# Local attention in a two-layer decoder trunk: the probabilities' transposes placed later among the products, the second head's further behind the first's

## The chip, the cores and the metric

The kernel runs as one program on 1 core of a Trainium2 chip. The time is that of the device in microseconds (us). Three runs of the kernel before gave 1879.4, 1879.95 and 1882.35 us, a median of 1879.95 us; a fourth run was taken with the hardware profiler, and all rows quoted here are from that execution.

## The reference

A decoder trunk of two layers over 16 meta tokens and 512 tokens, width 1024, in float32. Each layer is a half-step SwiGLU feed-forward net, a token mixer and another half-step feed-forward net, each between two RMS norms. Layer 0 mixes by gated linear attention, layer 1 by sliding-window attention with one set of keys and values. Only the latter is touched here:

```python
q = (hn @ w_q).reshape(B, L, N_KV_HEADS, GROUP, HEAD_DIM)      # 16 heads of 64
...
s = jnp.einsum('bkgnqd,bknsd->bkgnqs', q_blk, k_band)          # band: 16 meta, 128 previous, 128 own keys
...
p = sink_softmax(s, mask, sink_b[None, :, :, None, None, None])
o_real = jnp.einsum('bkgnqs,bknsd->bkgnqd', p.astype(v.dtype), v_band)
...
return o @ w_out
```

## The kernel before, in words

**Data.** Activations lie transposed (128 channels on the partitions, 528 tokens along the free axis, 8 such tiles for 1024 channels). A product against a weight is made of three float32r products (high and low halves, `mm3s`), weights arrive by DMA in pieces of 128x512 (`raw`), and each piece is split into its halves by ScalarE (L237) and VectorE (L238). PSUM is one pool of 8 tiles of 128x512 (`pp`), so every new product needs a tile whose last reader is done.

**An order written by a planner.** Python generators write the program. `Flow` keeps a clock that only the products advance, by an estimate of each one's time (`mm`, `transpose`); after each group of three products `flow.pump()` runs the generators that are due on that clock, and `yield t` in a generator means "go on when the clock is t further". A number in a `yield` is therefore a place among the products of TensorE, not a time on the chip. The scheduler of the framework then orders each engine's instructions, and may move a few of them past each other. Each engine runs its own list strictly in order.

**Sliding-window attention (`swa`, layer 1).** The 16 heads are 8 pairs, u = 0 to 7; the two heads of a pair are e = 0 and 1. For each pair:

- `x_first` and `x_units` make the queries q; pairs 0 to 3 come together, pairs 4 to 7 one after the other in TensorE tiles `x210` to `x213` (24 products each). VectorE and GpSimd rotate them (`rope`, L1035 to L1038).
- `soft(u)`: for four blocks b of 128 queries the scores of both heads (`sc<u>_<e><b>`, 128x144 for b = 0, else 128x272), moved to SBUF with mask and row minimum by VectorE (L1149), exponentials with row sums on ScalarE (L1156). Then `yield SOFT`, the sinks' part (`es`, L1158, L1159), the reciprocal of the sums (L1161, L1162) and the normalising products: the meta columns of both heads on VectorE (`mt`, L1169), the first head's probabilities on VectorE, the second head's on GpSimd (L1172).
- `core(u)`: `yield NORM`, then for each head eight or seven transposes of 128x128 on TensorE (L177) into two PSUM tiles (`pt<u>_<e>` and `pp<u>_<e>`), copied to SBUF by ScalarE (L1191) and VectorE (L1192), and a `yield` after each head; a last `yield 0.6`; then 22 products with the values into one tile `o<u>`, which is split into halves by ScalarE and VectorE (L398, L399).

A pair's `core` starts when its `soft` is done; `soft(u)` waits for `soft(u - 2)`, and from u = 4 on also for `core(u - 3)`. Between these, TensorE has `x211` to `x213` as other work while pairs 0 to 3 run, and the first half of the output projection (`out_proj(so[:4])`, tiles `y`) as soon as the cores 0 to 3 are done; the second half needs cores 4 to 7.

Of the kernel before, what the change touches and what calls it, by code (L numbers as in the profile page):

```python
# [46 lines left out]
WIN = 2 * P + META  # L47
STAGGER = 5.0
SOFT = 3.0
NORM = 3.0  # L50
GAP = 2.2
LAG = 3
NEG = -1e30
# [74 lines left out]
def trunk_kernel(ctx: ExitStack, tc, a, out):  # L128
# [18 lines left out]
    def ps(name):  # L147
        return pp.tile([P, 512], F32, tag="ps", name=name)

    def pair_tile(name, dt=F32R):  # L150
        return hp.tile([P, 2, TOK], dt, tag="pair", name=name)
# [12 lines left out]
    def mm(o, lhs, rhs, start=True, stop=True, onto=False):  # L164
        inst = pe.matmul(o, lhs, rhs, start=start, stop=stop, skip_group_check=onto)  # L165
        n = 1
        for d in rhs.shape[1:]:
            n *= d
        flow.clock += n / 2400 if rhs.dtype == F32R else max(n / 600, 0.12)
        return inst  # L170
# [5 lines left out]
    def transpose(o, src):  # L176
        pe.transpose(o, src, ident)  # L177
        flow.clock += 0.12
# [217 lines left out]
    def split(dst, src, g):  # L396
        o, n = g
        act.activation(dst[:, 0, o : o + n], src, AF.Copy)  # L398
        dve.tensor_tensor(dst[:, 1, o : o + n], src, dst[:, 0, o : o + n].bitcast(F32), op=ALU.subtract)  # L399
# [695 lines left out]
    def swa(x, kv, finish):  # L1095
        kz, vt, vmz = kv
        set_ahead(10)
        with tc.tile_pool(name="ap", bufs=1) as ap:
# [75 lines left out]
            def core(u):  # L1174
                yield softs[u]
                yield NORM
                j = u // 4
                ss, mt = probs[u]
                pt = [pair_tile(f"pt{u}_{e}", F32) for e in range(2)]
                ptm = pt[0][:, 1, 384:512]  # L1180
                pts = []
                for e in range(2):
                    p, p2 = ps(f"pt{u}_{e}"), ps(f"pp{u}_{e}")
                    for b in range(4):
                        transpose(p[:, b * P : (b + 1) * P], ss[e][0][b][:, -P:])
                    for b in range(3):
                        transpose(p2[:, b * P : (b + 1) * P], ss[e][0][b + 1][:, :P])
                    if e == 0:
                        transpose(p2[:, 384:], mt.rearrange("p c m -> p (c m)"))
                    n = 384 if e else 512  # L1190
                    act.activation(pt[e][:, 0, :512], p, AF.Copy)  # L1191
                    dve.tensor_copy(pt[e][:, 1, :n], p2[:, :n])  # L1192
                    pts.append([pt[e][:, i, :m].rearrange("p (b c) -> p b c", c=P) for i, m in ((0, 512), (1, 384))])
                    yield 0.8
                yield 0.6
                o = ps(f"o{u}")
                kvh = [slice((2 * j + e) * 64, (2 * j + e) * 64 + 64) for e in range(2)]
                for b in range(4):
                    oo = [o[64 * e : 64 * e + 64, b * P : (b + 1) * P] for e in range(2)]
                    for e in range(2):  # L1200
                        mm(oo[e], vt[:, b, kvh[e]], pts[e][0][:, b], True, False)
                    for e in range(2):
                        mm(oo[e], vmz[j][:, 4 * e + b], ptm, False, b == 0)
                    for e in range(2 if b else 0):
                        mm(oo[e], vt[:, b - 1, kvh[e]], pts[e][1][:, b - 1], False, True)
                so[u] = pair_tile(f"so{u}")
                split(so[u], o, (META, SEQ))
# [4 lines left out]
            def attend(u, *after):  # L1212
                softs.append(flow.spawn(soft(u, [*after, *softs[max(u - 2, 0) : max(u - 1, 0)]])))
                cores.append(flow.spawn(core(u)))
# [185 lines left out]
```

## Time and profile before

| | |
|---|---|
| median of three runs | 1879.95 us |
| the profiled execution | 1878.16 us |
| its span on the core | 1876.4 us |
| TensorE busy | 1848.5 us (99%) |
| VectorE busy | 1358.9 us (72%) |
| ScalarE busy | 1002.8 us (53%) |
| GpSimd busy | 324.5 us (17%) |
| scores of the first pair begin | 1388.1 us |
| last products with the values begin | 1485.1 us |

The span is counted from the first to the last instruction; 1.76 us of the profiled execution lie around it. The shares are means over all stages. The change touches the stretch from about 1405 to 1485 us, where pairs 0 to 7 go through softmax and transposes, so that stretch is what has to be read. In rows of the timeline, a float32 product shows as two instructions, so 22 products of `o` are 44 rows, and a pair of score products is "x4".

### The profile page before, as it was taken

The page shows a single profiled execution, that of the slowest core. Times are in us where ns is not written, and L with a number is a line of the kernel's source. Part 1 is how long each engine was busy: PE and PEld are TensorE (multiplying, and loading weights), DVE is VectorE, ACT ScalarE, POOL GpSimd, SP SyncE. Part 2 cuts the span into 40 slices and gives each one's busy share as a digit, 9 for nine tenths or more (in the row PEclk, how much of TensorE's full clock was granted, in tenths as well). Part 3 has the DMA queues.
Part 4 walks back from the last instruction along what each step waited for, and adds up shares of the span by engine and source line. Part 5 has one row for each costly group of instructions (what it writes and reads, how often), then busy time and mean ns, then how long its engine had stood idle before and what let it go on. Part 6 is the DMA issues. An engine that isn't in the chain of part 4 may idle for free.

```text
span 1876.4 us, 36945 instructions
## 1 busy us (share of the span) xinstructions
PE 1848.5 (99%) x14218; PEld 1768.2 (94%) x14218; DVE 1358.9 (72%) x2681; ACT 1002.8 (53%) x2181; POOL 324.5 (17%) x378
## 2 busy tenths in 40 slices
PE   8999999999999999999999999999999999999997
PEld 8999999999999999999999898989976898989897
DVE  7884748776574988484789685858799589848584
ACT  6662636564455666262665563636556566636363
POOL 2101010320001310101033001010353131010102
PEclk9999999999999999999999999999999999999999
DMA  5555566322113255555642356565311215656551
GB/s 194 145 154 141 152 149 160 119 68 79 46 58 112 68 131 157 138 148 148 168 159 57 101 153 157 149 156 165 123 57 46 79 46 132 166 147 160 144 147 45
DMA packets 133104, 231.17 MB, mean 123 GB/s; under 512 B 14912, under 2 KB 27584, under 8 KB 132928
## 3 DMA queue, kind: packets, MB, share of 16 engines
q1 hardware_dynamic: 111904, 190.94, 32.3%
q0 software_dynamic: 20736, 37.76, 12.9%
q8 instruction: 111, 1.82, 0.4%
q14 instruction: 65, 0.53, 0.1%
q10 hardware_dynamic: 288, 0.13, 0.0%
HBM read 226.67 MB, written 2.10 MB: 122 GB/s over the span
## 4 chain that ended last, share of the span: by engine, by line
PE 89%; DVE 7%; ACT 2%; issue 1%; POOL 0%; DMA 0%; DVEq 0%; ACTq 0%; POOLq 0%
PE y L165 30%; PE a L165 21%; PE x L165 18%; PE c L165 10%; PE d L165 5%; PE e L165 1%; PE po L165 1%; DVE w L238 1%; PE o L165 1%; DVE H L457 1%; ACT s L1156 0%; PE ps L165 0%; ACT w L237 0%; DVE s L1149 0%; DVE sh_q L1035 0%
## 5 line engine op out<-in xcount | busy, mean ns | idle before, releaser
L270 POOL DMA_DIRECT2D raw<-in_w_in x144 | 126.0, 939 | 973.4 <-DMA raw<-in_w_in 429.4
L165 PE MATMUL y<-hidl0f,w 128*128 128x256 f32 (+1 forms) x2112 | 260.5, 285 | 0.0
L238 DVE TENSOR_TENSOR w<-raw,w 128x512 fp32r<-128x512 f32 x378 | 244.7, 675 | 20.8 <-ACT w L237 18.0
L165 PEld LDWEIGHTS y<-hidl0f,w 128*128 128x128 f32 x2112 | 258.7, 188 | 0.2
L265 DVE TENSOR_TENSOR w_s<-raw,w_s 128x512 fp32r<-128x512 f32 x288 | 195.2, 689 | 80.7 <-ACT w_s L264 78.5
L165 PE MATMUL y<-hidl1f,w 128*128 128x512 f32 (+1 forms) x1344 | 249.0, 346 | 0.0
L165 PEld LDWEIGHTS y<-hidl1f,w 128*128 128x128 f32 x1344 | 212.3, 188 | 33.2 <-DVE w L238 0.3
L264 ACT ACTIVATE w_s<-raw 128x512 fp32r<-128x512 f32 x288 | 177.6, 625 | 111.1 <-DVE raw L280 70.2
L237 ACT ACTIVATE w<-raw 128x512 fp32r<-128x512 f32 x378 | 207.5, 586 | 33.8 <-PE y L165 28.0
L265 DVE TENSOR_TENSOR w<-raw,w 128x512 fp32r<-128x512 f32 x216 | 145.6, 688 | 35.9 <-ACT w L264 34.1
L165 PE MATMUL x<-x_l0m,w 128*128 128x272 f32 (+1 forms) x1200 | 157.8, 288 | 0.0
L264 ACT ACTIVATE w<-raw 128x512 fp32r<-128x512 f32 x216 | 130.6, 621 | 48.0 <-PE y L165 42.2
L587 DVE TENSOR_TENSOR Y<-y,Y 128x256 f32<-128x256 f32 (+2 forms) x176 | 82.1, 473 | 100.4 <-PE y L165 100.1
L165 PEld LDWEIGHTS x<-x_l0m,w 128*128 128x128 f32 x1200 | 149.3, 188 | 1.2
L165 PE MATMUL a<-zl0f_t,w_s 128*128 128x264 f32 x864 | 117.4, 285 | 0.0
L165 PE MATMUL a<-zl1f_t,w_s 128*128 128x256 f32 x864 | 114.3, 281 | 0.8 <-ACT c L783 0.7
L394 POOL TENSOR_TENSOR acc_post<-acc_post,sq_post 128x256 f32<-128x256 f32 (+1 forms) x78 | 65.9, 844 | 282.6 <-ACT sq_post L393 280.2
L165 PEld LDWEIGHTS a<-zl0f_t,w_s 128*128 128x128 f32 x864 | 110.3, 188 | 0.0
L165 PEld LDWEIGHTS a<-zl1f_t,w_s 128*128 128x128 f32 x864 | 106.9, 188 | 1.9 <-ACT c L783 1.8
L165 PE MATMUL x<-x_l0f,w 128*128 128x256 f32 (+1 forms) x768 | 98.2, 289 | 7.6 <-ACT w L237 5.9
L165 PEld LDWEIGHTS x<-x_l0f,w 128*128 128x128 f32 x768 | 96.1, 191 | 8.6 <-ACT w L237 5.9
L165 PE MATMUL x<-x_l1f,w 128*128 128x256 f32 (+1 forms) x576 | 92.3, 320 | 0.0
(368 smaller groups left out, 3319.0 us busy)
## 6 DMA issues: line engine op xcount, KB each, us to landing
raw<-in_w_in SPq DMA_DIRECT2D x424, 256.0 KB, 3.8
raw<-in_w_in POOLq DMA_DIRECT2D x144, 256.0 KB, 5.2
raw<-in_w_out SPq DMA_DIRECT2D x96, 256.0 KB, 3.5
raw<-in_gla_in SPq DMA_DIRECT2D x50, 256.0 KB, 3.2
raw<-in_w_last SPq DMA_DIRECT2D x48, 256.0 KB, 3.5
raw<-in_w_out SPq DMA_DIRECT2D x64, 128.0 KB, 3.0
raw<-in_gla_out SPq DMA_DIRECT2D x16, 256.0 KB, 2.8
raw<-in_w_q SPq DMA_DIRECT2D x16, 256.0 KB, 4.2
```

What stands on the lines that cost most here:

```text
L165: inst = pe.matmul(o, lhs, rhs, start=start, stop=stop, skip_group_check=onto)
L237: act.activation(w[:, 0, :m], raw[:, :m], AF.Copy)
L238: hold(dve.tensor_tensor(w[:, 1, :m], raw[:, :m], w[:, 0, :m].bitcast(F32), op=ALU.subtract))
L264: act.activation(w[:, 0, :512], src, AF.Copy)
L265: dve.tensor_tensor(w[:, 1, :512], src, w[:, 0, :512].bitcast(F32), op=ALU.subtract)
L270: pool.dma_start(dst, src, accum_op=ALU.add)
L394: pool.tensor_tensor(sums[0][:, :n], sums[0][:, :n], t[:, :n], op=ALU.add)
L457: dve.tensor_tensor(h, t, h, op=ALU.add)
L587: dve.tensor_tensor(y, p[:, :n], y, op=ALU.add)
```

## The change

Two numbers of the planner change.

```diff
-NORM = 3.0
+NORM = 4.0
...
                     pts.append([pt[e][:, i, :m].rearrange("p (b c) -> p b c", c=P) for i, m in ((0, 512), (1, 384))])
-                    yield 0.8
+                    yield 0.7 if e else 2.0
                 yield 0.6
```

The first transposes of a pair are placed 1.0 us of planned products later, the second head's 2.0 instead of 0.8 behind the first's, and the products with the values 1.3 instead of 1.4 behind those: 2.1 us of planned products later in all. No instruction is added or removed.

On TensorE, pair 0, before: right behind the last product of the query tile x212 come its first head's transposes.

```order
L165 MATMUL x212_0_17271<-x_l1m_7_16760,w211_1_17268 128x512 x3
L177 MATMUL pt0_0_17372<-ident_73,Y_71 128x128 x4
L177 MATMUL pp0_0_17373<-ident_73,Y_71 128x128 x3
L177 MATMUL pp0_0_17373<-ident_73,mt0_17203 128x128
L165 MATMUL sc2_02_17386<-kz0_12392,q2_17069 128x272
L165 MATMUL sc2_12_17388<-kz0_12392,q2_17069 128x272
L177 MATMUL pt0_1_17405<-ident_73,Y_71 128x128 x4
L177 MATMUL pp0_1_17406<-ident_73,Y_71 128x128 x3
L165 MATMUL sc3_00_17422<-kz0_12392,q2_17069 128x144
```

The same place in the changed kernel, from the same product on:

```order
L165 MATMUL x212_0_17271<-x_l1m_7_16760,w211_1_17268 128x512 x3
L165 MATMUL x213_0_17380<-x_l1m_0_16596,w212_0_17216 128x512 x3
L165 MATMUL sc2_02_17386<-kz0_12392,q2_17069 128x272
L165 MATMUL sc2_12_17388<-kz0_12392,q2_17069 128x272
L177 MATMUL pt0_0_17394<-ident_73,Y_71 128x128 x4
L177 MATMUL pp0_0_17395<-ident_73,Y_71 128x128 x3
L177 MATMUL pp0_0_17395<-ident_73,mt0_17203 128x128
L165 MATMUL sc2_03_17421<-kz0_12392,q2_17069 128x272
L165 MATMUL sc2_13_17423<-kz0_12392,q2_17069 128x272
L165 MATMUL sc3_00_17433<-kz0_12392,q2_17069 128x144
L165 MATMUL sc3_10_17435<-kz0_12392,q2_17069 128x144
L165 MATMUL x213_0_17380<-x_l1m_1_16620,w212_0_17216 128x512 x3
```

Products of x213 and a pair of scores now stand ahead of the first head's transposes, and two pairs of scores and three products of x213 between the two heads'. Since x213 begins here, it is used up earlier. On TensorE before, the transposes of pair 2 stand among products of x213:

```order
L177 MATMUL pp2_0_17575<-ident_73,mt2_17336 128x128
L165 MATMUL x213_0_17538<-x_l1m_2_16640,w212_0_17216 128x512
L177 MATMUL pt2_1_17592<-ident_73,s2_1_17332 128x128 x4
L177 MATMUL pp2_1_17593<-ident_73,s2_1_17332 128x128 x3
L165 MATMUL x213_0_17538<-x_l1m_3_16665,w212_0_17216 128x512 x3
L165 MATMUL x213_0_17538<-x_l1m_4_16690,w212_1_17307 128x512 x3
L165 MATMUL x213_0_17538<-x_l1m_5_16710,w212_1_17307 128x512 x3
```

In the changed kernel they stand among scores of pair 4, and pair 3's first transposes follow ahead of o2:

```order
L177 MATMUL pp2_0_17602<-ident_73,mt2_17336 128x128
L165 MATMUL sc4_00_17638<-kz1_12393,q4_17167 128x144
L165 MATMUL sc4_10_17640<-kz1_12393,q4_17167 128x144
L165 MATMUL sc4_01_17646<-kz1_12393,q4_17167 128x272
L165 MATMUL sc4_11_17648<-kz1_12393,q4_17167 128x272
L177 MATMUL pt2_1_17652<-ident_73,s2_1_17332 128x128 x4
L177 MATMUL pp2_1_17653<-ident_73,s2_1_17332 128x128 x3
L165 MATMUL sc4_02_17665<-kz1_12393,q4_17167 128x272
L165 MATMUL sc4_12_17667<-kz1_12393,q4_17167 128x272
L177 MATMUL pt3_0_17673<-ident_73,s3_0_17427 128x128 x4
L177 MATMUL pp3_0_17674<-ident_73,s3_0_17427 128x128 x3
```

From the end of o1 to the end of o3 TensorE has no product of x213 any more, only scores, transposes and o2, o3; and three pairs of scores (pair 4, blocks 2 and 3, and pair 5, block 1) now stand ahead of the end of o3. The list of VectorE moves with it. Between the normalising of pair 3 (`s3_0`, `mt3`) and the first scores of pair 4 it now reads:

```order
L1172 TENSOR_TENSOR s3_0_17427<-s3_0_17427,den3_17430 128x816
L1169 TENSOR_TENSOR mt3_17432<-s3_1_17428,den3_17430 128x16
L1169 TENSOR_TENSOR mt3_17432<-s3_1_17428,den3_17430 128x48
L1035 STREAM_SHUFFLE sh_q7_16_17627<-x213_0_17380 128x512
L399 TENSOR_TENSOR so1_17596<-o1_17573,so1_17596 128x512
L1192 COPY pt2_0_17599<-pp2_0_17602 128x512
L1036 TENSOR_TENSOR q6_17374<-x213_0_17380,csq_16792 128x512
L1149 ISA s4_0_17632,nm4_17634<-sc4_00_17638,away_16788,nsink_16790 128x144
```

Before, both copies of pair 2 and the split of o1 stood ahead of that normalising, and the splits of two weight pieces (w216) behind it; now it is the other way round. GpSimd's and the DMA queue's lists keep their work: the rotation of pair 6 comes one pair of normalising products earlier on GpSimd, and the loads of weights keep their sequence.

## The prediction

> **What bounds the kernel now.** I began with the page's first part, engine by engine, and went from there to the stretch that the change touches.
>
> ```profile
> PE 1848.5 (99%) x14218; PEld 1768.2 (94%) x14218; DVE 1358.9 (72%) x2681; ACT 1002.8 (53%) x2181; POOL 324.5 (17%) x378
> ```
>
> TensorE (PE) is busy for 99% of the span, so a change of order that adds no instruction can only win or lose TensorE's idle time. The table by stretches (width, then busy time of PE, of its weight loads, of VectorE = DVE, ScalarE = ACT and GpSimd = POOL, then the granted clock) cuts where the program cuts: from the first transposes of pair 0 to the end of o3, from there to the end of o7, and the rest of the output projection.
>
> ```profile
> 1405.40:1438.60 33.20, 29.50 (x298) 22.91 (x296) 30.28 (x93) 18.50 (x59) 14.71 (x12) 1.00 0.16 49
> 1438.60:1485.30 46.70, 45.94 (x371) 35.04 (x370) 31.95 (x106) 27.20 (x83) 7.73 (x8) 1.00 0.11 35
> 1485.30:1512.00 26.70, 26.70 (x212) 25.97 (x211) 17.64 (x38) 16.37 (x35) 9.27 (x12) 1.00 0.32 100
> ```
>
> TensorE is idle for 33.20 - 29.50 = 3.70 us in the first stretch, 0.76 us in the second and not at all in the third: 4.46 us in all, 0.24% of the span. The view of waits says for what:
>
> ```profile
> PE pt L177 <- DVE s L1172: 1.7, 3, 0.9
> PE pt L177 <- POOL s L1172: 0.8, 1, 0.8
> PE pt L177 <- POOL Y L1172: 0.7, 1, 0.7
> PE pp L177 <- ACT pt L1191: 0.5, 1, 0.5
> PE o L165 <- DVE pt L1192: 0.5, 1, 0.5
> PE pt L177 <- DVE nm L1149: 0.2, 1, 0.2
> ```
>
> Nearly all is transposes that wait for normalised probabilities, which later transposes could avoid. But the first stretch has a second reading. DVE is busy for 30.28 us of 33.20 there, and its rows (start, length, operation, idle time ahead) show that it never rests until pair 3 is normalised:
>
> ```profile
> 1410.04 0.68 DVE L238 TENSOR_TENSOR w<-raw,w 128x512 fp32r<-128x512 f32 x1
> 1410.64 0.19 DVE L1162 RECIPROCAL den<-den 128x8 f32<-128x8 f32 x1
> ...
> 1416.68 0.68 DVE L1192 COPY pt<-pp 128x512 f32<-128x512 f32 x1
> ...
> 1418.12 0.55 DVE L1192 COPY pt<-pp 128x384 f32<-128x384 f32 x1
> ...
> 1424.19 0.68 DVE L399 TENSOR_TENSOR so<-o,so 128x512 fp32r<-128x512 f32 x1
> ...
> 1428.29 1.00 DVE L1172 TENSOR_TENSOR s<-s,den 128x816 f32<-128x816 f32 x1
> ...
> 1432.52 0.69 DVE L399 TENSOR_TENSOR so<-o,so 128x512 fp32r<-128x512 f32 x1 [2.40 <-ACT so L398]
> ```
>
> The first idle time is the 2.40 us ahead of 1432.52. So **VectorE sets the pace from 1405 to about 1430 us**, and TensorE's waits there are its queue seen from the other side. Two rows next to each other run into one another by 0.08 us (0.68 from 1410.04, the next at 1410.64), so I count a row's length less 0.08 as its cost.
>
> **The change, part by part.** No instruction comes or goes, and the loads keep their sequence; the cost is waits alone. I follow the changed lists in three steps, against the profiled execution.
>
> *Step 1: when VectorE has normalised pair 3.* Before, at 1428.29 + 1.00 = 1429.29. Ahead of that point the changed list holds two splits of weights more (0.60 each, row 1410.04), and does without pair 2's two copies (0.60 and 0.47, rows 1416.68 and 1418.12) and one split of o1 (0.60, row 1424.19): +1.20 - 1.67 = -0.47. VectorE would be there at 1428.8 if it stays as busy as it was.
>
> *Step 2: when TensorE reaches pair 3's transposes.* Its rows give the price of each piece:
>
> ```profile
> 1405.42 0.63 PE L177 MATMUL pt<-ident,Y 128*128 128x128 f32 x4
> ...
> 1426.91 2.32 PE L165 MATMUL x<-x_l1m,w 128*128 128x512 f32 x9
> 1429.16 0.44 PE L165 MATMUL o<-pt,vt 128*64 128x128 f32 x4
> ...
> 1459.21 0.52 PE L165 MATMUL sc<-kz,q 64*128 64x144 f32 x4
> 1459.66 0.97 PE L165 MATMUL y<-so,w 128*128 128x512 f32 x3
> 1460.56 0.44 PE L165 MATMUL o<-pt,vt 128*64 128x128 f32 x4
> ...
> 1463.11 0.73 PE L165 MATMUL sc<-kz,q 64*128 64x272 f32 x4
> 1463.77 0.66 PE L177 MATMUL pt<-ident,s 128*128 128x128 f32 x4
> ...
> 1464.79 0.73 PE L165 MATMUL sc<-kz,q 64*128 64x272 f32 x4
> 1465.45 0.66 PE L177 MATMUL pt<-ident,s 128*128 128x128 f32 x4
> ...
> 1466.37 0.73 PE L165 MATMUL sc<-kz,q 64*128 64x272 f32 x4
> ```
>
> From start to next start: a query product 0.25 us (nine from 1426.91 to 1429.16), a pair of scores 0.66 (1463.11 to 1463.77) or 0.45 for block 0, transposes of a first head 1.02, of a second 0.92, the 22 products of an o 2.55 (1460.56 to 1463.11). Before, from 1405.42 to the end of o3, these give 24 x 0.25 + 6 x 0.66 + 3 x 0.45 + 4 x 1.94 + 4 x 2.55 = 29.3 us, against 29.50 in the table: the prices hold. In the changed list, between the same start and pair 3's first transposes, stand all 24 products of x213 (6.0), seven pairs of scores and two of block 0 (5.5), the transposes of pairs 0, 1 and 2 (5.8), o0 and o1 (5.1): 22.4 us, so without a wait TensorE would come there at 1427.8. The probabilities are there at 1428.8, and the PSUM tile that these transposes get is one from which VectorE must first have moved pair 4's block 0. The rows for what VectorE does in between:
>
> ```profile
> 1405.37 0.28 DVE L1169 TENSOR_TENSOR mt<-Y,den 128x16 f32<-128x16 f32 x2
> ...
> 1434.34 0.73 DVE L1035 STREAM_SHUFFLE sh_q<-x 128x512 f32<-128x512 f32 x1
> ...
> 1435.48 0.68 DVE L1036 TENSOR_TENSOR q<-x,csq 128x512 f32<-128x512 f32 x1
> 1436.07 0.36 DVE L1149 CUSTOM_DVE_ANT_0 s<-sc,away,nsink 128x144 f32<-128x144 f32 x1
> ...
> 1437.22 0.50 DVE L1149 CUSTOM_DVE_ANT_0 s<-sc,away,nsink 128x272 f32<-128x272 f32 x1
> ```
>
> That is mt 0.20, shuffle 0.65, split of o1 0.60, copy 0.60, rotation 0.60 and two scores 0.57: 3.2 us, to 1432.0. TensorE thus idles for 1432.0 - 1427.8 = **4.2 us instead of 3.70** by then, however the waits are spread: +0.5. Bounds: if the tile comes free elsewhere, 1428.8 decides, 1.0 us of idle, or -2.7; if VectorE itself is held up, later by as much. I take the tile, since the list names that order.
>
> *Step 3: after that.* Behind them stand 1.0 + 2.55 (o2) + 0.66 + 0.92 + 0.45 + 0.66, and o3. VectorE's next copies fit: pair 2's second copy is due at 1432.0 + 0.84 (two scores at 0.42) + 0.47 = 1433.3, o2 starts at 1433.0 and reads it after nine of its 22 products (1.0 us); pair 3's last copy comes about as o3 starts. I count nothing. Past o3, products of the output projection stand among the scores and transposes, and VectorE has 31.95 us of work in 46.70. The 0.76 us of the second stretch (transposes of pairs 4 and 5 next to each other) should go, as pairs 4 and 5 now stand apart: **-0.7**, at worst 0. Behind o7 stand 12 products of the first half of the projection instead of 15: 12 x 0.25 = 3.0 us, and nine small ones, still more than the 1.2 us that the split of o7 takes (0.60 on VectorE by the row of 1424.19, and I take as much for ScalarE): nothing, and 1.2 us if that cover were gone.
>
> The sum is +0.5 - 0.7 = -0.2 us on the profiled execution's 1878.16. That execution is 1.8 us under the median of the runs, so against the median: 1879.95 - 0.2, **about 1879.7 us**. No change that can be measured.
>
> **The rivals.** All turn on VectorE, whose cost is not fixed:
>
> ```profile
> 1411.37 1.22 DVE L1172 TENSOR_TENSOR Y<-Y,den 128x144 f32<-128x144 f32 x2
> ...
> 1416.61 0.15 DVE L1158 TENSOR_TENSOR es<-nm,vec 128x8 f32<-128x8 f32 x1
> ...
> 1420.81 1.02 DVE L1169 TENSOR_TENSOR mt<-s,den 128x16 f32<-128x16 f32 x2
> 1421.75 2.31 DVE L1172 TENSOR_TENSOR s<-s,den 128x144 f32<-128x144 f32 x2
> ...
> 1424.79 1.45 DVE L1158 TENSOR_TENSOR es<-nm,vec 128x8 f32<-128x8 f32 x1
> ```
>
> ```profile
> 1424.29 1.94 POOL L1172 TENSOR_TENSOR s<-s,den 128x144 f32<-128x144 f32 x2 [1.09 <-DVE mt L1169]
> ```
>
> The same tiny es took 0.15 and 1.45 us; the long one ended at 1426.24, when GpSimd's pair of products ended (1424.29 + 1.94 = 1426.23). The normalising pair took 1.22 and 2.31, mt 0.28 and 1.02, each time beside GpSimd. The excess of these three is 1.30 + 1.09 + 0.74 = 3.1 us.
>
> *Faster.* If the new order puts GpSimd's products beside VectorE's copies and scores out of PSUM, that excess goes, VectorE is 3.1 us earlier, the tile decides at 1428.9, and 1.1 us of idle are left: 3.70 - 1.1 = 2.6, with 0.76 behind it 3.4 us, 1876.5; at most all 4.46 us, 1875.5. For it: every wait of the list above is one that a later transpose avoids. Against it: GpSimd has five pairs of products in this stretch either way, and x213's products, that covered pair 2's waits, are spent earlier.
>
> *Slower.* The same holding-up hits VectorE more often. From o1 to o3 TensorE now has no query product, so each us that VectorE is late there is a us on o3. Four more waits like es's at 1424.79 cost 4 x 1.30 = 5.2 us: 1884.9. It decides from three on (3.9 us). For it: rotation and normalising of GpSimd now follow closer on each other. Against it: one row in the old stretch is that bad.
>
> The Trainium skill, "SBUF — State Buffer", section "Who interferes with whom", says that a VectorE instruction with two SBUF inputs is blocked for a whole GpSimd instruction that reads SBUF, while one with at most one SBUF input is not. The rows agree for es; the rule adds that copies out of PSUM are safe, by which the faster rival would be possible, with the same 1876.5.
>
> Against the change speaks "TensorE: Matmul & The Clock Gate" of the Trainium skill, section "What's actually happening": after an idle window of about 3.4 us the clock falls to half. If the 4.2 us of idle came in one piece, an estimate from that page is 1.7 us more, 1881.4. The longest wait in the view above is 0.9 us, with a granted clock of 1.00, and no row shows such a fall.
>
> *That the change does not do what it says* is out: the lists show the moves.
>
> **How the numbers follow.** What a measurement of this kernel can tell from no change is about 0.2%, 3.8 us. My forecast has 0.70, the faster rival 0.18, the slower one 0.12. The faster rival's 1876.5 lies just within 0.2%, its far end at 1875.5 beyond: I give it 0.10 beyond and 0.08 within. So faster by more has 0.10, slower by more 0.12, and within 0.2% 0.78. The range reaches from all idle time gone, 1879.95 - 4.46 = 1875.5, up to three more waits on VectorE, 1879.7 + 3.9 = 1883.6; runs of the kernel before spread by 3 us, so that a part of either rival lies outside.
>
> **What would show it.** Right: in the new profile TensorE is idle for 4 to 5 us from x212's end to o3's, mostly ahead of o0, and of pair 3's transposes, released by DVE's pt (L1192) or nm (L1149) instead of s (L1172); o3 ends near 1440.7; TensorE never waits behind it. Wrong: VectorE with idle time ahead of pair 3's normalising (step 1), normalising long before 1428 or behind 1430 (the rivals), or waits behind o3 (step 3).

## The result, and the profile after

| | before | after |
|---|---|---|
| median of 22 runs each | 1879.05 us (1877.36 to 1882.35) | 1875.9 us (1875.54 to 1877.89) |
| ratio | | 0.9984, 95% interval 0.9979 to 0.999 |
| the profiled execution | 1878.16 us | 1875.54 us |
| the stage (first score product to first product of the next net, `x_l1f`) | 123.88 us | 121.76 us |
| ahead of the stage, unchanged code | 1388.10 us | 1387.50 us |

The change wins 3.1 us between the medians, 0.16%: within 0.2% by the medians, though the interval reaches 0.21%, and not zero. Between the two profiled executions it is 2.62 us, of which 2.12 are in the stage and 0.6 ahead of it, where the code is the same (about 0.1 goes the other way behind it); in all profiles below the stage starts at 1387.4 to 1388.5 whatever the kernel, so I compare stages. For the rest of the 3.1 the clock is the likely cause; the section on the prediction says how far that is shown.

The page's first part after:

```profile
PE 1849.6 (99%) x14218; PEld 1768.5 (94%) x14218; DVE 1354.6 (72%) x2681; ACT 1003.5 (54%) x2181; POOL 323.2 (17%) x378
```

TensorE is busy for 1.1 us more and VectorE for 4.3 us less, with the same instructions. The table by stretches, cut at the same points of the program as in the prediction (the end of `x212`, the end of o3, the end of o7):

```profile
1404.80:1439.32 34.52, 33.62 (x310) 24.67 (x308) 32.20 (x107) 22.57 (x70) 13.37 (x12) 1.00 0.18 55
1439.32:1483.35 44.03, 44.03 (x363) 34.39 (x361) 27.57 (x93) 24.39 (x72) 7.73 (x8) 1.00 0.11 31
1483.35:1509.30 25.95, 25.95 (x209) 25.36 (x208) 17.36 (x38) 15.73 (x34) 9.22 (x12) 1.00 0.31 103
```

TensorE's idle time is 34.52 - 33.62 = 0.90 us, and then none; before it was 3.70 and 0.76. What it waits for in this part:

```profile
PE sc L165 <- DVE q L1036: 0.7, 1, 0.7
PE pt L177 <- DVE pt L1192: 0.2, 1, 0.2
```

No wait for a normalised probability (DVE s, POOL s, POOL Y) is left. The first stretch is now the longer one because work moved into it: 12 pairs of scores stand in it instead of nine. Over the whole stage (width, then TensorE busy), before and after:

```profile
1388.10:1511.98 123.88, 117.94 (x951) 93.68 (x950) 96.98 (x294) 73.85 (x216) 42.22 (x42) 1.00 0.20 63
```

```profile
1387.50:1509.26 121.76, 119.36 (x951) 94.20 (x951) 94.25 (x294) 74.44 (x216) 40.79 (x42) 1.00 0.21 64
```

TensorE's idle time fell from 5.94 to 2.40, by 3.54 us, while its busy time rose by 1.42: together the 2.12. So not all of the idle time that went was won. VectorE did the same 294 rows in 2.73 us less. Cut at the end of o3, with the three pairs of scores that moved counted at 0.66 us each (1.98 us), the part of the stage ahead of it became 0.65 us shorter and the part behind it 1.46: two thirds of the gain lie where pairs 4 to 7 are worked on.

### The profile page after: what moved, and what is told of

It reads as the page before. It is cut to its first block, busy times and chain, and to the rows that moved or that the text cites. A ratio compares the mean times of both kernels' runs of the same rounds, so it can differ in the third digit from the quotient of the medians.

```text
span 1873.7 us, 36947 instructions
## 1 busy us (share of the span) xinstructions
PE 1849.6 (99%) x14218; PEld 1768.5 (94%) x14218; DVE 1354.6 (72%) x2681; ACT 1003.5 (54%) x2181; POOL 323.2 (17%) x378
## 4 chain that ended last, share of the span: by engine, by line
PE 91%; DVE 6%; ACT 2%; issue 1%; DMA 0%; POOL 0%; SPq 0%; DVEq 0%; ACTq 0%; POOLq 0%
PE y L165 30%; PE a L165 22%; PE x L165 18%; PE c L165 10%; PE d L165 5%; PE o L165 1%; PE e L165 1%; PE po L165 1%; DVE w L238 1%; PE sc L165 1%; DVE H L457 1%; PE ps L165 0%; PE pt L177 0%; ACT w L237 0%; DVE Y L587 0%
```

## The experiments

Two theories. **L (hold-up):** VectorE sets the pace of the stage, part of its time is holding still while GpSimd works, and the new order wins by putting GpSimd's products beside other rows. **P (place):** later transposes simply wait less; GpSimd has nothing to do with it. If GpSimd's products are taken out, L says the order wins next to nothing any more, P that it wins the same. Stages are from one profile of each. The kernels were timed in four groups, each on a chip of its own, with the kernel before beside them at 1878.32 (norm_only, gap_only, before_act, after_act), 1878.5 (before_nopool, after_nopool, after_pair, gap_pair), 1877.83 (gap_act, norm_act, after_again) and 1878.77 us (before_again).

| kernel | median us | ratio to before, interval | stage us |
|---|---|---|---|
| norm_only | 1876.8 | 0.999 (0.9982 to 0.9999) | 122.22 |
| gap_only | 1875.33 | 0.9987 (0.9978 to 0.9996) | 121.04 |
| before_act | 1874.99 | 0.9982 (0.9973 to 0.9991) | 121.31 |
| after_act | 1878.05 | 0.9999 (0.999 to 1.0008) | 123.98 |
| before_nopool | 1874.26 | 0.9978 (0.9969 to 0.9986) | 120.31 |
| after_nopool | 1874.03 | 0.9974 (0.9964 to 0.9984) | 122.19 |
| after_pair | 1877.16 | 0.9994 (0.9985 to 1.0003) | 122.54 |
| gap_pair | 1878.88 | 0.9999 (0.999 to 1.0008) | 124.57 |
| gap_act | 1874.49 | 0.9978 (0.9969 to 0.9988) | 120.34 |
| norm_act | 1876.02 | 0.999 (0.9981 to 0.9998) | 122.54 |
| after_again | 1875.84 | 0.9985 (0.9976 to 0.9994) | 121.77 |
| before_again | 1878.15 | 0.9998 (0.9989 to 1.0007) | 127.36 |

### The two halves of the change alone

norm_only has the pair's later start, gap_only the second head's later place:

```diff
-NORM = 3.0
+NORM = 4.0
```

```diff
-                    yield 0.8
+                    yield 0.7 if e else 2.0
```

> Only NORM = 4.0; the gap between a pair's two heads stays at 0.8. Theory P (place: a transpose that stands later waits less, whatever GpSimd does): each of the two edits brings its share of planned time, 1.0 of 2.1 us, so about -1.5 us of the change's -3.1 us in the medians, and the idle time of TensorE from the first transposes to the end of o7 falls from 4.46 us to about 2.5. Theory L (lock: the time is won where GpSimd's products no longer stand beside VectorE's operations on SBUF): no share is due; the time follows the excess of VectorE's rows (es over 0.15, normalising pair over 1.22, mt over 0.28 us), and may be nothing or the whole.

> Only the second head's transposes further behind the first's (2.0 and 0.7 instead of 0.8 and 0.8); NORM stays at 3.0. Theory P: the share of the other 1.1 of 2.1 us, about -1.6 us, TensorE idle about 2.5 us. Theory L: as the excess of VectorE's rows beside GpSimd goes, nothing or the whole; the two parts need not add up to the change.

Measured: the second head's place alone wins 3.0 us (stage -2.84), the pair's later start alone 1.5 us (stage -1.66), both together 3.1 (stage -2.12). Theory P's figure came for the later start (-1.5) and not for the other (-1.6 expected). The halves do not add up: they cure the same loss, and `NORM` on top of the other costs 0.7 us of stage. The second head's place is the part that wins more. It does not do so by less hold-up in total: VectorE is busy for 94.96 us of norm_only's stage and 95.00 of gap_only's, and the stages differ by 1.18 us. Which row is held, and whether TensorE waits behind it, matters too.

### The second head normalised on ScalarE instead of GpSimd

In both kernels, the second head's product of each block with its reciprocal becomes an activation with a scale (four for a pair):

```diff
-                        (pool if e else dve).tensor_tensor(tt, tt, dv.to_broadcast([P, n, w]), op=ALU.mult)
+                        if e == 0:
+                            dve.tensor_tensor(tt, tt, dv.to_broadcast([P, n, w]), op=ALU.mult)
+                        for c in range(b, b + n if e else b):
+                            act.activation(ss[e][0][c], ss[e][0][c], AF.Identity, scale=den[:, e, c : c + 1])
```

> The kernel before, with the second head's probabilities normalised on ScalarE (four activations per pair) instead of GpSimd: GpSimd has only the two rotations left in the stretch. Theory L: VectorE's excess beside GpSimd (1.30 + 1.09 + 0.74 us in three rows) is gone and the kernel gains 2 to 3 us on the kernel before. Theory P: the transposes still stand too early and wait for VectorE; within 1 us of the kernel before, or slower by ScalarE's additional 15 us of work in a stretch of 80.

> The changed kernel with the same move to ScalarE. Theory L: without the lock the change has nothing left to win: within 0.7 us of the run with the order of before and the same move. Theory P: the change is worth its 2 us here as well: 1.5 us or more faster than that run.

before_act wins 2.57 us of stage with the planner's places of before, more than the change does, and 3.3 us in the medians; L had said 2 to 3. after_act is a miss for it: 3 us slower than before_act, no faster than the kernel before. Its waits say part of why:

```profile
PE o L165 <- ACT pt L1194: 1.0, 1, 1.0
PE sc L165 <- ACT pt L1194: 0.5, 1, 0.5
PE sc L165 <- DVE q L1036: 0.3, 1, 0.3
```

TensorE now waits for ScalarE's copies of transposes (`pt`), which stand in ScalarE's list behind the second heads' activations. ScalarE is busy for 85.70 us of this stage instead of 74.44. The waits are not the whole of it: against before_act's stage TensorE's idle time is up by only 0.65 us, its busy time by 2.02, and after_act's timeline shows pairs of scores split between the two heads, each of which costs more (see step 2 below). So the test was not clean: it took one load away and put another in the way. And with the move to ScalarE the scheduler ordered some products of x213 and of o, and some transposes, differently, in before_act as in after_act. Two things followed, leaving the products out without a substitute, and trying each half with ScalarE.

### The second head's products left out

These two kernels leave out the normalising of the second head (the same edit without the activations), so that neither GpSimd nor ScalarE does it. In the stage, TensorE and VectorE run the same sequence of operations as in the kernel before and in the changed kernel.

```diff
-                        (pool if e else dve).tensor_tensor(tt, tt, dv.to_broadcast([P, n, w]), op=ALU.mult)
+                        if e == 0:
+                            dve.tensor_tensor(tt, tt, dv.to_broadcast([P, n, w]), op=ALU.mult)
```

> The kernel before, with the second head's normalising products on GpSimd left out (they are on no other engine either; the second head's probabilities stay unnormalised). Neither GpSimd's lock nor ScalarE's additional work is there. Theory L (the change wins because VectorE is held up 2 to 3 us less beside GpSimd): 2 to 3 us less than the kernel before, as with the move to ScalarE. Theory W (the waits of the transposes for data are what the change removes): the two first-head waits (1.7 us) remain, so at most 1.5 us less than before, from the second heads' 1.5 us.

> The changed kernel with the same products left out. Theory L: within 0.7 us of the order of before with the same omission, or slower than it by what the change costs on TensorE (one pair of scores split by a product of x213, 0.65 us). Theory W: 1.5 to 2 us faster than that run.

The stages (width, TensorE busy, weight loads, VectorE busy) of before_nopool, and then after_nopool:

```profile
1387.40:1507.71 120.31, 116.96 (x950) 93.76 (x950) 91.99 (x294) 73.56 (x216) 25.07 (x26) 1.00 0.21 65
```

```profile
1387.50:1509.69 122.19, 120.28 (x951) 95.02 (x950) 91.55 (x294) 74.28 (x216) 24.74 (x26) 0.99 0.21 64
```

The medians differ by 0.23 us, 1874.26 and 1874.03: without GpSimd's products the order wins nothing that shows. (The longer stage of after_nopool holds a fall of the granted clock, which its 0.99 tells and the last section shows; from the query products at 1389.95 to the twelve score products behind them it is 5.12 us, and 3.59 in the changed kernel. That costs 1.5 us, and 122.19 - 1.5 = 120.7 stands against 120.31.) Theory P is refuted as it was put: the change does not win the same without GpSimd's products. Leaving them out of the order of before wins 4.2 us in the medians and 3.57 of stage, more than L's 2 to 3 and far more than the 1.5 that theory W allowed; in the changed order it shortens the stage by about 1.1 (121.76 to 120.7). The same rows measure the hold-up. VectorE's 294 rows take 96.98 us before and 91.99 without the products, so it was held for 4.99 us; after the change 94.25 - 91.55 = 2.70 are left. The order took away 2.3 us of hold-up, and the stage became 2.12 us shorter; that the two are so alike is not shown to be more than chance, as norm_only and gap_only tell.

One rival these runs do not part from the hold-up. Ahead of o3 the second heads' transposes waited for GpSimd's results themselves (0.7 and 0.8 us in the view of waits before), and leaving the products out takes that wait away as well. How much of the gain ahead of o3 is this direct wait stays open; behind o3 no transpose waits for GpSimd, and step 3 below shows the hold-up there.

### Keeping a pair's score products together

Rows of the new order show some score products of one head alone. Theory S: that split costs time, and ordering the next product behind the pair's second score would win it back. The edit, in after_pair on the changed kernel and in gap_pair on gap_only, is an ordering between two instructions, in `mm` and in `soft`:

```diff
+    scored = [None]
...
+        if scored[0] is not None:
+            after(scored[0], inst)
+            scored[0] = None
...
-                        mm(pst[e][:, :n], qq[rows, META + b * P : META + (b + 1) * P], keys[rows, k0 : k0 + n])
+                        last = mm(pst[e][:, :n], qq[rows, META + b * P : META + (b + 1) * P], keys[rows, k0 : k0 + n])
+                    scored[0] = last
```

> The changed kernel, with the next product ordered behind a pair's second score product, so that the scheduler cannot put a product of x213 between the scores of the two heads (sc3_01 and sc3_11). Theory S (a lone head's score product takes as long as both heads' together, 0.65 us, so a split pair costs 0.65): 0.6 us less than the changed kernel. Rival: the second head's product waits for its PSUM tile just as long, and the time is the same within 0.3 us.

> Only the gap between the heads (NORM = 3.0, 2.0 and 0.7), with the same ordering. Theory S: 0.6 us less than gap_only, about 1874.7 us, the fastest so far. Rival: the same as gap_only within 0.3 us.

S does not hold as a gain: after_pair's stage is 0.78 us longer than the changed kernel's, and its median 1.3 us above that of the changed kernel, which was timed in another group. TensorE's busy time in the stage falls by 0.5 us (119.36 to 118.84), and waits take more than that:

```profile
PE sc L167 <- DVE q L1041: 0.7, 1, 0.7
PE pt L182 <- DVE pt L1198: 0.7, 1, 0.7
PE sc L167 <- DVE nm L1155: 0.4, 1, 0.4
PE o L167 <- DVE nm L1155: 0.4, 1, 0.4
```

By these waits, the split was the scheduler filling a wait for VectorE with something. gap_pair is 3.5 us slower than gap_only, and in its profile nearly all of that is the clock; the last section shows it.

### The halves with ScalarE, and the changed kernel again

gap_act is before_act with the second head's place, norm_act is before_act with `NORM` 4.0 (edits as above), and after_again is the changed kernel, timed beside them.

> The kernel before, with the later place of the second head's transposes (0.7 and 2.0 in place of 0.8) and with the second head normalised on ScalarE instead of GpSimd; NORM stays at 3.0. Theory L (what the change wins is VectorE's hold-up beside GpSimd's products): with those products gone the place wins nothing more, so within 0.7 us of before_act's 1875.0, first score to next net's first product near 121.3 us. Rival Q (with ScalarE as the loaded engine a later place of the second head leaves its transposes and copies behind ScalarE's next activations): 1.5 to 3 us slower than before_act, 1876.5 to 1878, with TensorE waiting for ACT pt and DVE q. Rival P (the place by itself wins): 1 us or more below 1875.0.

> The kernel before, with NORM 4.0 alone and with the second head normalised on ScalarE instead of GpSimd. Theory L: within 0.7 us of before_act's 1875.0. Rival Q, if it is the pair's later start and not the second head's place that loads ScalarE badly: 1.5 us or more slower, 1876.5 to 1878. If gap_act is slow and this is not, the slowness of after_act lies in the second head's place; if neither is, in the two together.

> The changed kernel itself once more, beside the two others, so that all are compared on one chip: 1875.9 us, 3 us below the kernel before. Its profile is a second one of the same code: by theory L the stage from the first score to the next net's first product takes 121.8 us again, within 0.3, unless the granted clock falls behind one of its waits.

gap_act's median is 0.5 us below before_act's, within L's 0.7; but before_act was timed in another group, whose kernel before was 0.5 us slower too, so that against the kernel before the two win the same 3.3 us. Its stage is 0.97 us shorter. norm_act is 1.0 us slower than before_act (stage +1.23), between L's 0.7 and the 1.5 of rival Q, and waits 0.9 us for ScalarE's `pt` ahead of an o, as after_act does. So Q's wait is there with the pair's later start, not with the second head's place, and both halves together are worse (stage +2.67) than their sum. With GpSimd's products the second head's place wins 2.84 us of stage, with ScalarE in their stead 0.97: about two thirds of its gain hang on GpSimd's products, through the hold-up or the direct wait, and the rest is place or the scheduler's different order. after_again repeats the stage to 0.01 us.

**gap_act has the shortest stage of all versions that compute everything; its median is 1.35 us below that of the changed kernel beside it.** Its stage:

```profile
1388.00:1508.34 120.34, 118.69 (x951) 94.11 (x951) 92.12 (x294) 84.87 (x248) 24.91 (x26) 1.00 0.21 65
```

TensorE is idle there for 120.34 - 118.69 = 1.65 us, 1.5 of it in one wait that ends at 1390.5, where the change does not reach.

### The kernel before, profiled again

> The kernel before itself, for a second profile. Its 22 times so far fall into two parts, 1877.4 to 1878.4 and 1878.8 to 1882.4, while the changed kernel's lie nearly all in 1875.4 to 1876.4. Theory H (the granted clock falls to half for one or two stretches of 3.4 us behind the worst waits of the stage, in some executions of it): a profile whose time is over 1879 shows a clock of about 0.5 somewhere in 1386 to 1435 us and a stage as much longer, and one under 1878.5 shows 1.00 throughout and a stage of 123.9 us. Rival (the spread comes from elsewhere, from the loads): a profile over 1879 with a clock of 1.00 in the stage, longer in the lead ahead of it. Theory L says nothing on this; it takes the stage's 2.1 us between the two profiles at 1.00 as what the order wins, and the rest of the 3.1 us between medians as H's.

The profile fell on an execution of 1881.12 us. The table by 5 us (the granted clock is the number ahead of the last two) shows theory H right:

```profile
1385.00:1390.00 5.00, 3.57 (x18) 2.37 (x16) 5.00 (x17) 0.00 (x0) 4.04 (x6) 1.00 0.00 0
1390.00:1395.00 5.00, 4.93 (x13) 3.25 (x13) 3.77 (x11) 2.06 (x8) 4.84 (x5) 0.66 0.56 154
...
1425.00:1430.00 5.00, 3.67 (x18) 3.14 (x19) 4.44 (x12) 1.93 (x4) 1.93 (x2) 0.77 0.00 0
1430.00:1435.00 5.00, 5.00 (x55) 4.09 (x54) 2.08 (x6) 0.12 (x1) 3.20 (x2) 0.89 0.18 56
```

Twice the clock falls behind a stretch with idle time. Its rows at the two places:

```profile
1390.07 3.68 PE L165 MATMUL x<-x_l1m,w 128*128 128x512 f32 x8 [1.50 <-DVE w L238]
...
1427.65 0.90 PE L177 MATMUL pt<-ident,s 128*128 128x128 f32 x3 [0.83 <-POOL s L1172]
1428.35 0.85 PE L177 MATMUL pp<-ident,s 128*128 128x128 f32 x3
1428.85 3.37 PE L165 MATMUL x<-x_l1m,w 128*128 128x512 f32 x9
```

The nine products of 1428.85 took 2.32 in the first profile (the row of 1426.91 in the prediction), the eight of 1390.07 took 2.13 there. From 1390.07 to the twelve score products that follow it is 5.16 us instead of 3.60, and from 1427.65 to the next products with the values 4.50 instead of 2.88: each fall costs 1.6 us, together 3.2 of the 3.48 by which this stage is longer than the first profile's.

## Why the prediction was right where it was, and wrong where it was not

The forecast was 1879.7 us, -0.2 against the median shown then; the change gives -3.1. "Within 0.2%" and the range hold, the likeliest case does not. That "within 0.2%" holds is no merit of the sum, which had the change at nothing: a gain of 3.1 us also lies within 3.8. It is nearly the faster rival's 1876.5 that came.

**What bounds the kernel: right.** VectorE sets the pace up to pair 3's normalising: with TensorE's list as it was, leaving GpSimd's products out shortens VectorE's busy time by 4.99 us and the stage by 3.57 (before_nopool). It is not the only thing that moves the time: gap_act's stage is 0.97 us shorter than before_act's, with VectorE busy as long (92.12 and 92.15 us).

**Step 1 failed**, at the words "if it stays as busy as it was". Pair 3 was to be normalised at 1428.8. To set the changed profile on the clock of the one before I add 0.62 us (the end of `x212`, 1405.42 against 1404.80). VectorE's rows after that show what I had left as it was:

```profile
1410.57 0.80 DVE L1161 TENSOR_TENSOR den<-den,es 128x8 f32<-128x8 f32 x1
...
1414.92 1.00 DVE L1158 TENSOR_TENSOR es<-nm,vec 128x8 f32<-128x8 f32 x1
...
1424.52 0.59 DVE L1158 TENSOR_TENSOR es<-nm,vec 128x8 f32<-128x8 f32 x1
1425.44 0.17 DVE L1161 TENSOR_TENSOR den<-den,es 128x8 f32<-128x8 f32 x1 [0.34 <-ACT es L1159]
...
1426.09 1.23 DVE L1172 TENSOR_TENSOR s<-s,den 128x144 f32<-128x144 f32 x2
```

Pair 3's products end at 1427.3, or 1427.9 on the clock of before: 0.9 us earlier. The normalising pair takes 1.23 and not 2.31, and `mt` never 1.02. Other rows are held instead, shorter: `den` 0.80 against 0.17, es 1.00 and 0.59 against 0.15. Each of the three ends with a GpSimd row:

```profile
1410.06 1.29 POOL L1038 TENSOR_TENSOR q<-q,sh_q 128x512 f32<-128x512 f32 x1
1413.97 1.93 POOL L1172 TENSOR_TENSOR Y<-Y,den 128x144 f32<-128x144 f32 x2 [2.63 <-DVE mt L1169]
1423.00 2.08 POOL L1172 TENSOR_TENSOR s<-s,den 128x144 f32<-128x144 f32 x2 [7.10 <-DVE mt L1169]
```

1410.06 + 1.29 = 1411.35 and 1410.57 + 0.80 = 1411.37; 1415.90 and 1415.92; 1425.08 and 1425.11. In the whole stage the groups shift in the same way, first before, then after (busy time, mean ns of one):

```profile
L238 DVE TENSOR_TENSOR w<-raw,w 128x512 fp32r<-128x512 f32 x29 | 23.7, 832 | 0.7 <-ACT w L237 0.7
...
L1169 DVE TENSOR_TENSOR mt<-s,den 128x16 f32<-128x16 f32 x12 | 4.1, 344 | 0.1
...
L1161 DVE TENSOR_TENSOR den<-den,es 128x8 f32<-128x8 f32 x8 | 1.2, 162 | 1.7 <-ACT es L1159 1.7
```

```profile
L238 DVE TENSOR_TENSOR w<-raw,w 128x512 fp32r<-128x512 f32 x29 | 21.8, 772 | 0.5 <-ACT w L237 0.5
...
L1161 DVE TENSOR_TENSOR den<-den,es 128x8 f32<-128x8 f32 x8 | 3.1, 392 | 1.5 <-ACT es L1159 1.4
...
L1169 DVE TENSOR_TENSOR mt<-s,den 128x16 f32<-128x16 f32 x12 | 2.1, 172 | 0.2
```

The splits of weights take 1.9 us less and `mt` 2.0 less, `den` 1.9 more. The rule that I weighed from the Trainium skill ("SBUF — State Buffer", "Who interferes with whom") thus holds in every row looked at. The faster rival, which had 0.18, named this mechanism, and nearly its idle time ahead of o3 (1.1 us left, measured 0.90). That its 1876.5 lies so near the result is partly luck: ahead of o3 most of the idle time that went came back as busy time, so that 0.65 us were won there instead of its 2.6; behind o3 1.46 were won instead of its 0.76; and about 1.0 of the 3.1 us between the medians lies outside the stage's 2.12. I argued against it that GpSimd has five pairs of products in this stretch either way. It has four (and two rotations), and the argument is beside the point, since what counts is which VectorE row falls beside them.

**Step 2: the kind of wait was named rightly, the places and the size were not.** TensorE does wait behind VectorE's list, but ahead of a score of pair 3 (0.69 us) and of pair 1's transposes (0.18), not ahead of o0 or of pair 3's transposes, and shortly. TensorE's rows after:

```profile
1407.30 1.27 PE L165 MATMUL sc<-kz,q 64*128 64x272 f32 x6
1409.26 0.51 PE L165 MATMUL sc<-kz,q 64*128 64x144 f32 x2 [0.69 <-DVE q L1036]
...
1411.36 0.72 PE L165 MATMUL sc<-kz,q 64*128 64x272 f32 x2
...
1412.51 0.72 PE L165 MATMUL sc<-kz,q 64*128 64x272 f32 x2
...
1429.51 1.21 PE L165 MATMUL sc<-kz,q 64*128 64x272 f32 x4
1430.65 0.66 PE L177 MATMUL pt<-ident,s 128*128 128x128 f32 x4
```

Pair 3's transposes begin at 1430.65, 1431.27 on the clock of before, instead of 1432.0; o3 ends at 1439.32, or 1439.9, instead of 1440.7. Of the 4.2 us of idle that I had by then only 0.90 show, and yet the end of o3 came only 0.8 us earlier than forecast, since TensorE's rows became longer: products of one head alone (x2) take 0.72, as long as both heads' together (x4, 0.73), so a pair whose heads are split costs about 0.65 more, and in the row of 1429.51 (1.21 where a pair costs 0.73) the second head starts only at 1430.00. TensorE is busy for 33.62 us in this part; the 29.50 of before and three more pairs of scores at 0.66 would be 31.48. My prices had no term for these 2.1 us, and after_pair shows that they can't simply be had back.

**Step 3: right that the wait goes, half the size, and another cause.** Nothing waits behind o3, as I said. From o3's end to the end of the stage it took 73.38 us before, and 69.94 after. Three pairs of scores less at 0.66 are 1.98 of the difference; 1.46 are the gain, against the 0.7 that I took. The 0.76 was read from the view of waits, and the rows of the transposes of pairs 4 and 5 before show what that view leaves out:

```profile
1451.14 0.33 PE L177 MATMUL pt<-ident,s 128*128 128x128 f32 x1
1451.66 0.55 PE L177 MATMUL pt<-ident,s 128*128 128x128 f32 x3 [0.19 <-DVE s L1172]
...
1453.92 0.55 PE L177 MATMUL pp<-ident,s 128*128 128x128 f32 x3 [0.49 <-ACT pt L1191]
1454.39 0.73 PE L165 MATMUL sc<-kz,q 64*128 64x272 f32 x4
```

From 1451.14 to 1454.39 are 3.25 us for the transposes of a first and a second head, which cost 1.94 where nothing waits: 1.31 lost, of which 0.68 stand as idle. Instructions that trickle in one by one count as busy. I put this wait down to pairs 4 and 5 standing next to each other. It came from a held row again, `mt` of pair 5 beside GpSimd's products of pair 4 (two such rows take 0.28 or 0.29 us where nothing holds them):

```profile
1448.82 1.64 DVE L1169 TENSOR_TENSOR mt<-s,den 128x16 f32<-128x16 f32 x2
...
1448.38 1.93 POOL L1172 TENSOR_TENSOR s<-s,den 128x144 f32<-128x144 f32 x2 [10.60 <-DVE mt L1169]
```

In before_nopool, where the two pairs stand next to each other as before, TensorE has no idle time behind o3, and from o3's end to the end of the stage it takes 72.03 us, 1.35 less than before. In the changed order a `den` is held there for 1.35 us (at 1451.10), and TensorE does not wait behind it.

Of the signs that I had named, "TensorE never waits behind it" came, and o3 near 1440.7 nearly; 4 to 5 us of idle did not, and VectorE has idle time ahead of pair 3's normalising (0.34 us at 1425.44), which I had named as the sign against step 1.

**The clock: dismissed too early.** I weighed "TensorE: Matmul & The Clock Gate" of the Trainium skill ("What's actually happening") as speaking against the change, and set it aside because no row showed such a fall. The one profile that I had was of an execution without one in this stage. In before_again it falls at two places of the stage, behind 1388 and behind 1424, and the change takes the second one's idle time away. Of the 22 times of before, ten lie at 1877.4 to 1878.4 and twelve at 1878.8 to 1882.4; of the changed kernel's, 19 lie at 1875.5 to 1876.3. Between the medians of the two lower parts (1877.74 and 1875.77) there are 2.0 us, close to the stage's 2.12; the other 1.1 us of the 3.1 would be that the upper part has become rarer. The two falls are shown for one execution of before; that falls make up the whole upper part is argued from the times, not shown.

## What to carry to other kernels

When one engine sets the pace and some of its rows take several times their usual length, price a change of order with the rows' undisturbed lengths and as a second case with the hold-up elsewhere, and do not carry the hold-up of the old order over as a constant. Take the length of a waiting piece from start to start of its neighbours, not from the idle time that the view of waits shows. And before 1.5 us of idle time within 3.4 us are called cheap, look at the spread of several runs' times: it can hold a fall of the clock that one profile doesn't show.

## What the runs showed of the hardware

**Half the clock without a whole idle window.** In gap_pair TensorE waited 0.24 and 1.12 us, and was still busy for 2.26 us of the 3.41 ahead of the fall. The table at the fall (the granted clock is the third number from the end), then rows around it:

```profile
1409.83:1413.24 3.41, 2.26 (x11) 1.24 (x11) 3.41 (x16) 1.63 (x6) 0.17 (x1) 1.00 0.55 146
1413.24:1420.03 6.79, 6.58 (x36) 4.84 (x38) 6.72 (x24) 4.83 (x16) 4.27 (x4) 0.50 0.13 38
```

```profile
1413.45 1.27 PE L167 MATMUL sc<-kz,q 64*128 64x272 f32 x2 [1.12 <-DVE nm L1155]
1414.65 1.11 PE L182 MATMUL pt<-ident,Y 128*128 128x128 f32 x4
1415.56 0.85 PE L182 MATMUL pp<-ident,Y 128*128 128x128 f32 x3
```

Four transposes take 1.11 us instead of 0.66 until 1420.03, 6.79 us later; at half speed that is about 3.4 us lost, which is gap_pair's difference to gap_only. In the second profile of before each fall lasted 3.4 us (from about 1390.1 to 1393.5 and from 1427.7 to 1431.1), and the starts lie 37.6 us apart, eleven times 3.42. The page of the Trainium skill that I cited ("TensorE: Matmul & The Clock Gate", "What's actually happening") speaks of windows of about 3.4 us that run freely, and the lengths agree. It names an idle window as what brings the fall; if that means one without any work, these traces do not agree: TensorE was busy for 56% to 66% of the 3.4 us ahead of the falls (1.90 and 1.91 of 3.40 us in before_again, 1.93 in after_nopool, 2.26 of 3.41 in gap_pair). The same idle time, 1.5 us near 1389, stands in every profile here, and the clock fell behind it in two of them (after_nopool, before_again). In the first profile of before, 1422.7 to 1426.1 was busy for only 1.83 of 3.40 us, and no fall came behind it. That is how it would be if it depended on where the window's edge lies; the runs don't show the edge itself.

**Two heads at the price of one.** Score products whose operands fill 64 rows run side by side for the two heads of a pair: x4 (both heads) takes 0.73 us and x2 (one) 0.72. I had not priced that a split pair costs twice.

**The smallest rows can be held the longest.** A 128x8 `es` or `den` of 0.15 to 0.17 us took up to 1.45 us before (1424.79) and 1.35 after (1451.10), and ended with a pair of GpSimd's products (1426.23 and 1452.43).
